# Scores of gated linear attention: three four-way decay steps and a diagonal step with conditional copies, in place of seven two-way levels

## The chip, the core and the metric

The kernel runs on one core of one Trainium2 chip. The metric is device time in microseconds (us). The kernel before takes 827.52 us, the median of three runs (826.87 to 828.48).

Six engines or queues matter here. TensorE is PE, and its weight loads have a row of their own, PEld. VectorE is DVE, ScalarE is ACT and GpSimd is POOL. SyncE is SP, and all large loads are issued from its queue. Each works through its own list of instructions in order, and they meet at semaphores.

## The reference, cut to what matters

One layer of a decoder trunk, 256 tokens wide, model width 2048. `h = RMSNorm(x)` is multiplied by one wide projection, and three attention branches read the parts of the result. Each branch is gated, projected, merged, projected once more and added to x. The part that the change touches is the first branch, gated linear attention (GLA), 4 heads of 128 key dimensions, in chunks of tokens:

```python
b = jnp.cumsum(gi, axis=2)                                   # cumulative log decay, per key dimension
diff = b[:, :, :, None, :] - b[:, :, None, :, :]
decay = jnp.exp(jnp.where(causal[None, None, :, :, None], diff, -jnp.inf))
scores = jnp.einsum('bhid,bhjd,bhijd->bhij', qi, ki, decay)  # for key j <= query i
o_intra = jnp.einsum('bhij,bhje->bhie', scores, vi)
```

A score is the sum over d of q[i,d] k[j,d] exp(b[i,d] - b[j,d]). The exponent depends on i, j and d together, so a plain matmul can't form it. Where a reference token r lies between j and i, the exponential splits in two factors that are both at most 1: exp(b[r] - b[j]) goes to the key and exp(b[i] - b[r]) to the query, and a matmul over d then gives the score.

## The kernel before, in words

**Projections.** The weights are 34 blocks of 2048 x 512, all in fp32. A block is read in four quarters of 1 MB (`w_quarter`, load L129) into one of three buffers named `raw`. Each quarter is split in two halves, and of each half ACT writes the rounded part `hi` (L124) and DVE the remainder `lo` (L125). There are four `hi` and four `lo` buffers. PE then makes three matmuls per product (L166 to L168 for 512 columns, L181 to L184 for 256). One step over 128 of the 2048 rows is a "pull", and it has 6 such matmuls of 512 columns or 12 of 256. A `hi`/`lo` half lasts two pulls.

**Threading.** The attention work isn't a stage of its own. It is written as generators in two lanes, `main` and `side`. After each pull, each lane may emit one step, and a step says how many pulls it lasts. So the instructions of PE are projections with small islands of attention work in them. PE's and SP's instructions stand in the order of the program. For DVE, ACT and POOL a scheduler orders them when the kernel is built, and weights go first (`high_priority`). The `side` lane meanwhile brings the memory tokens: four loads `memT` (L253), split into `m` by ACT L247 and DVE L248, and four loads `memn` (L206) whose squares ACT sums (L207). These loads use the same three `raw` buffers as the weights.

**Scores before** (`gla_scores`). `gB` holds 16 times the cumulative log decay of both token tiles and 4 heads, as 128 dimensions by 1024. It comes from a scan on DVE (L415). `gq` and `gk` hold queries and keys in the same layout. First the scores between the two token tiles are made from `cd` (L448 to L453, matmul L468). The diagonal is a plain product q k of 128 x 128 for each of the 8 head tiles (L460), from which L461 keeps the diagonal. Then come seven levels with s = 64, 32, 16, 8, 4, 2, 1. At each level every 2s tokens are cut into two halves, the last token of the first half is the reference, and second-half queries meet first-half keys. `prep(s)` makes the keys `E` and queries `Q` (DVE L436, L437, ACT exponential L438, DVE L440, L443) one level ahead. PE makes 8 products of 64 columns (L478), DVE multiplies by a mask of 0 and the scale (L480), and adds the result to the score matrix `gA` (L483). A level lasts 11 pulls (`LEVEL_GAP`). After that `gla_out` multiplies the scores by the values (L497, L498).

**After the scores.** The main lane goes on with `gla_out`. The forgetting attention `fox` is put into the lane after the block `fv` is done, and `memory` after the block `mq`. All small matmuls of these parts are in fp32 and go through four PSUM banks named `att`.

Of the kernel before, what the change touches and what calls it, by code (L numbers as in the profile page):

```python
# [24 lines left out]
# columns of w_in  # L25
# [12 lines left out]
# the 512-column blocks in the order in which they are used: (matrix, first column)  # L38
# [9 lines left out]
# columns of the packed constants  # L48
# [6 lines left out]
LEVELS = (64, 32, 16, 8, 4, 2, 1)  # L55
# [4 lines left out]
def body(ctx, tc, xT, memT, xn, memn, wall, wsm, wup, cst, fgain, out):  # L60
# [11 lines left out]
    # the order of the tensor engine's and of the loads' instructions is that of the program  # L72
# [49 lines left out]
    # ------------------------------------------------ weights  # L122
# [34 lines left out]
    def natural(h, kts, wsrc):  # L157
        """psum[t] = h[:, t] @ block: two [128 tokens, 512] banks."""
# [13 lines left out]
    def transposed(h, wsrc, bank=acc):  # L172
        """psum[c] = block columns (tiles 2c, 2c+1) as partitions x 256 tokens."""
# [26 lines left out]
    def rms_of(src, col, stage):  # L200
        """col = rstd as columns [128, NT]."""
# [13 lines left out]
    def row_of(col, row):  # L215
        """row = rstd as a row on every partition [128, S]."""
# [9 lines left out]
    # ------------------------------------------------ constants  # L226
# [12 lines left out]
    # the tensor engine reaches its full clock while the first loads are under way  # L239
# [11 lines left out]
    def load_split(src, tag, gcol, g, h, raw, ks):  # L251
        """Token tiles ks of group g: the gain-scaled transposed input as an exact pair of parts."""
# [17 lines left out]
    def first_w():  # L270
        """The first block and the input with it, in pieces that grow."""
# [22 lines left out]
    xrow = cpool.tile([P, S], F32, name="xrow")  # L294
    mcol = cpool.tile([P, NT], F32, name="mcol")
# [3 lines left out]
    # ------------------------------------------------ the projections  # L299
# [21 lines left out]
    # ------------------------------------------------ constants for later  # L321
# [4 lines left out]
    # masks of the decay levels, carrying the scale of the scores  # L326
    gmask = cpool.tile([P, len(LEVELS), 64], F32, name="gmask")
    nc.gpsimd.memset(gmask, QS)
    for li, s in enumerate(LEVELS):
        nb = 64 // s  # L330
        mk_ = gmask[:, li, :].rearrange("p (b s) -> p b s", s=s)
        nc.gpsimd.affine_select(out=mk_, in_=mk_, pattern=[[-2 * s, nb], [0, s]],
                                compare_op=ALU.is_ge, fill=0.0, base=0, channel_multiplier=1)
        nc.gpsimd.affine_select(out=mk_, in_=mk_, pattern=[[2 * s, nb], [0, s]],
                                compare_op=ALU.is_ge, fill=0.0, base=s - 1, channel_multiplier=-1)
    gdiag = cpool.tile([P, P], F32, name="gdiag")
    nc.vector.tensor_scalar(gdiag, ident, QS, None, ALU.mult)
    # additive causal mask of the two query tiles: [tile 0 | keys 0 | keys 1]
# [7 lines left out]
    # ------------------------------------------------ the 24 small columns  # L346
# [14 lines left out]
    def small_and_norm():  # L361
        """The norm of x; the small columns; the first two blocks' evacuation."""
# [10 lines left out]
        G["q"] = evac_T(gq_ps, xrow)  # L373
# [7 lines left out]
    def log_sigmoid(*args):  # L381
        """dst = min(u, 0) - ln(1 + exp(-|u|)) for each (dst, u, tmp)."""
# [24 lines left out]
        # and the log forget gates of the 8 forgetting heads (rows 32..39)  # L407
# [17 lines left out]
    def gla_scores():  # L425
# [3 lines left out]

        def prep(s):  # L430
# [5 lines left out]
            nc.vector.tensor_tensor(out=Ev[:, :, 0, :], in0=ref, in1=Bv[:, :, 0, :], op=ALU.subtract)  # L436
            nc.vector.tensor_tensor(out=Ev[:, :, 1, :], in0=Bv[:, :, 1, :], in1=ref, op=ALU.subtract)  # L437
            nc.scalar.activation(E, E, AF.Exp, scale=1.0 / 16)  # L438
            Q = a2([P, 8, 64])
            nc.vector.tensor_tensor(out=Q.rearrange("p a (b s) -> p (a b) s", s=s), in0=Ev[:, :, 1, :],  # L440
                                    in1=gqf.rearrange("p (b u s) -> p b u s", u=2, s=s)[:, :, 1, :],
                                    op=ALU.mult)
# [29 lines left out]
        for li, s in enumerate(LEVELS):  # L472
            E, Q = nxt
            if li + 1 < len(LEVELS):
                nxt = prep(LEVELS[li + 1])
# [435 lines left out]
```

## Time and profile before

| what | value |
|---|---|
| median of 3 runs | 827.52 us (826.87 to 828.48) |
| span of the profiled execution, first to last instruction | 824.9 us |
| instructions profiled | 10985 |
| mean granted TensorE clock | 0.997 |
| DVE busy | 488.9 us (59%) |
| ACT busy | 400.5 us (49%) |
| POOL busy | 15.7 us (2%) |
| HBM | 154.39 MB read, 2.10 MB written, 190 GB/s over the span |

The runs shown are 2.6 us longer than the span at their median; the profiled execution has no time listed beside its span, and that difference lies ahead of the first instruction and behind the last. In a row of the timeline the first number is the start in us from the beginning of the span, the second how long the row lasted, and in brackets stands how long the engine had been idle before it and who ended that. On DVE and ACT consecutive instructions overlap a little, so the start-to-start distance is shorter than the duration. A PE row's duration is modelled and also longer than the distance to the next row. An fp32 matmul shows as two instructions ("passes").

### The profile page before, as it was taken

What the parts mean: (1) busy time and instruction counts of PE and PEld (TensorE: products, weight loads), DVE (VectorE), ACT (ScalarE), POOL (GpSimd) and SP (SyncE); (2) the same over time, 40 slices, a digit from 0 to 9 for tenths busy, and PEclk for the clock granted to TensorE, in tenths of its full rate; (3) what the DMA queues carried; (4) which work ended last, traced back from release to release, by engine and by line L of the source; (5) the groups of instructions that cost most, each with busy time, mean ns of one, the idle gap of its engine ahead of it and who ended that gap; (6) DMA issues with size and microseconds to landing.
All of it is one profiled execution on the core that took longest, in us unless ns stands there. A gap on an engine that the chain in (4) does not pass through costs nothing.

```text
span 824.9 us, 10985 instructions
## 1 busy us (share of the span) xinstructions
PE 814.3 (99%) x4470; PEld 708.0 (86%) x4470; DVE 488.9 (59%) x631; ACT 400.5 (49%) x515; POOL 15.7 (2%) x36
## 2 busy tenths in 40 slices
PE   9999999999999999999999999999999999999995
PEld 9998899989899778998888888888888888888885
DVE  6645999665546667666445744474446544566833
ACT  7736765643354456554444444434443444445611
POOL 4000300000000000000000000000000000000000
PEclk9999999999999999999999999999999999999998
DMA  8943466755534344445556545555555555576802
GB/s 316 390 151 125 147 236 226 265 199 165 193 130 173 108 153 154 146 162 182 182 197 204 202 163 197 204 194 170 198 204 194 169 199 204 196 268 249 303 2 103
DMA packets 27363, 157.22 MB, mean 191 GB/s; under 512 B 3216, under 2 KB 4640, under 8 KB 10416
## 3 DMA queue, kind: packets, MB, share of 16 engines
q1 hardware_dynamic: 27040, 156.48, 54.1%
q8 instruction: 35, 0.57, 0.3%
q14 instruction: 16, 0.13, 0.0%
q10 hardware_dynamic: 144, 0.02, 0.0%
q0 software_dynamic: 128, 0.02, 0.0%
HBM read 154.39 MB, written 2.10 MB: 190 GB/s over the span
## 4 chain that ended last, share of the span: by engine, by line
PE 96%; DMA 1%; SPq 1%; DVE 0%; ACT 0%; issue 0%; DVEq 0%; ACTq 0%
PE acc L166 19%; PE acc L168 19%; PE acc L167 19%; PE acc L181 7%; PE acc L183 7%; PE acc L184 7%; PE acc L804 4%; PE acc L803 4%; PE acc L802 4%; DMA raw<-wall 1%; PE att L478 1%; PE att L575 1%; PE att L567 0%; PE att L369 0%; PE att L594 0%; PE att L719 0%
## 5 line engine op out<-in xcount | busy, mean ns | idle before, releaser
L125 DVE TENSOR_TENSOR lo<-raw,hi 128x1024 fp32r<-128x1024 f32 (+2 forms) x269 | 323.3, 1204 | 263.6 <-ACT hi L124 263.5
L124 ACT CAST hi<-raw 128x1024 fp32r<-128x1024 f32 (+2 forms) x269 | 277.8, 1035 | 315.6 <-PE acc L168 214.6
L166 PE MATMUL acc<-hi,x 128*128 128x512 f32 x544 | 215.3, 396 | 0.0
L168 PE MATMUL acc<-hi,x 128*128 128x512 f32 x544 | 211.9, 390 | 0.0
L167 PE MATMUL acc<-lo,x 128*128 128x512 f32 x544 | 211.9, 389 | 0.0
L168 PEld LDWEIGHTS acc<-hi,x 128*128 128x128 f32 x544 | 102.1, 188 | 21.7
L166 PEld LDWEIGHTS acc<-hi,x 128*128 128x128 f32 x544 | 102.2, 188 | 20.9 <-issue 0.5
L167 PEld LDWEIGHTS acc<-lo,x 128*128 128x128 f32 x544 | 102.2, 188 | 20.4
L181 PE MATMUL acc<-x,hi 128*128 128x256 f32 x384 | 110.4, 287 | 0.0
L184 PE MATMUL acc<-x,lo 128*128 128x256 f32 x384 | 108.7, 283 | 0.0
L183 PE MATMUL acc<-x,hi 128*128 128x256 f32 x384 | 108.6, 283 | 0.0
L183 PEld LDWEIGHTS acc<-x,hi 128*128 128x128 f32 x384 | 73.7, 192 | 0.3
L181 PEld LDWEIGHTS acc<-x,hi 128*128 128x128 f32 x384 | 73.6, 192 | 0.3
L184 PEld LDWEIGHTS acc<-x,lo 128*128 128x128 f32 x384 | 73.6, 192 | 0.0
L166 PE MATMUL acc<-hi,oT 128*128 128x512 f32 x128 | 49.8, 389 | 0.0
L167 PE MATMUL acc<-lo,oT 128*128 128x512 f32 x128 | 49.8, 389 | 0.0
L168 PE MATMUL acc<-hi,oT 128*128 128x512 f32 x128 | 49.8, 389 | 0.0
L802 PE MATMUL acc<-hi,a 128*128 128x512 f32 x96 | 37.5, 391 | 0.0
L804 PE MATMUL acc<-hi,a 128*128 128x512 f32 x96 | 37.4, 389 | 0.0
L803 PE MATMUL acc<-lo,a 128*128 128x512 f32 x96 | 37.4, 389 | 0.0
L167 PEld LDWEIGHTS acc<-lo,oT 128*128 128x128 f32 x128 | 24.0, 188 | 5.0
L168 PEld LDWEIGHTS acc<-hi,oT 128*128 128x128 f32 x128 | 24.0, 188 | 5.0
(218 smaller groups left out, 860.2 us busy)
## 6 DMA issues: line engine op xcount, KB each, us to landing
raw<-wall SPq DMA_DIRECT2D x132, 1024.0 KB, 4.8
a<-xn SPq DMA_DIRECT2D x8, 512.0 KB, 7.7
raw<-wall SPq DMA_DIRECT2D x4, 512.0 KB, 7.7
raw<-memT SPq DMA_DIRECT2D x4, 512.0 KB, 3.9
raw<-memn SPq DMA_DIRECT2D x4, 512.0 KB, 5.1
out<-a SPq DMA_DIRECT2D x8, 256.0 KB, 3.2
raw<-wall SPq DMA_DIRECT2D x7, 256.0 KB, 4.3
a<-xT SPq DMA_DIRECT2D x8, 128.0 KB, 4.0
```

The source lines that it names most:

```text
L124: nc.scalar.copy(hi, src)
L125: nc.vector.tensor_tensor(out=lo, in0=src, in1=hi.bitcast(F32), op=ALU.subtract)
L166: MM(ps[t], lhsT=h1, rhs=hi, start=(kt == first), stop=False)
L167: MM(ps[t], lhsT=h1, rhs=lo, start=False, stop=False)
L168: MM(ps[t], lhsT=h2, rhs=hi, start=False, stop=(kt == last))
L181: MM(o, lhsT=w1, rhs=hk[:, 0, :], start=(kt == 0 and c % 2 == 0), stop=False, skip_group_check=True)
L183: MM(o, lhsT=w1, rhs=hk[:, 1, :], start=False, stop=False, skip_group_check=True)
L184: MM(o, lhsT=w2, rhs=hk[:, 0, :], start=False, stop=(kt == KT - 1), skip_group_check=True)
L478: MM(ps[:, e, :], lhsT=E[:, e * P:(e + 1) * P], rhs=Q[:, e, :], start=True, stop=True)
L802: MM(ps, lhsT=h1, rhs=hi, start=(kt == 0), stop=False)
L803: MM(ps, lhsT=h1, rhs=lo, start=False, stop=False)
L804: MM(ps, lhsT=h2, rhs=hi, start=False, stop=(kt == KT - 1))
```

## The change

The seven levels become three four-way steps, s = 32, 8, 2. At each step every 4s tokens are cut into four parts. Each of the first three parts has its last token as reference: its keys carry exp(b[end] - b[j]), and all later parts of the same 4s tokens are its queries. For a head tile of 128 tokens that makes 96 + 64 + 32 = 192 query columns (`Q_N`), in place of 64 at a level before. The keys `E` of all 128 tokens are one subtraction, one exponential and one product (L455, L458, L459 of the changed kernel). The queries are made in two tiles of four head tiles each: three differences (L466), one exponential (L470) and three products (L472) for each. A last step joins neighbours and the diagonal: 64 columns for the odd tokens with the decay from their left neighbour (L485 to L487), and 128 plain query columns, copied by POOL (L488); its keys are the plain `gk`.

A step is 8 products of 192 columns (L522), two to an `att` bank, so it takes all four banks. The scores aren't scaled, masked and added any more. The scale is in the queries already (`qrow`), and a conditional copy on DVE (`copy_predicated`, L536) writes the places where a mask of 0 and 1 is set into `gA`, which POOL has cleared (L503). A step has 12 such copies (4 banks, 3 parts of 192, 128 and 64 elements a partition), the last one 8. The steps still last 11 pulls, so that there are four of them in place of seven levels, and the diagonal's two groups before the first level are gone.

```diff
-LEVELS = (64, 32, 16, 8, 4, 2, 1)
+STEPS = (32, 8, 2)
+Q_OFF = (0, 96, 160)
+Q_N = 192
...
         def prep(s):
-            nb = 1024 // (2 * s)
-            Bv = gB.rearrange("p (b u s) -> p b u s", u=2, s=s)
             E = a4([P, 1024])
-            Ev = E.rearrange("p (b u s) -> p b u s", u=2, s=s)
-            ref = Bv[:, :, 0, s - 1:s].to_broadcast([P, nb, s])
-            nc.vector.tensor_tensor(out=Ev[:, :, 0, :], in0=ref, in1=Bv[:, :, 0, :], op=ALU.subtract)
-            nc.vector.tensor_tensor(out=Ev[:, :, 1, :], in0=Bv[:, :, 1, :], in1=ref, op=ALU.subtract)
+            Bv = gB.rearrange("p (b s) -> p b s", s=s)
+            nc.vector.tensor_tensor(out=E.rearrange("p (b s) -> p b s", s=s),
+                                    in0=Bv[:, :, s - 1:s].to_broadcast([P, 1024 // s, s]), in1=Bv,
+                                    op=ALU.subtract)
             nc.scalar.activation(E, E, AF.Exp, scale=1.0 / 16)
-            Q = a2([P, 8, 64])
-            nc.vector.tensor_tensor(out=Q.rearrange("p a (b s) -> p (a b) s", s=s), in0=Ev[:, :, 1, :],
-                                    in1=gqf.rearrange("p (b u s) -> p b u s", u=2, s=s)[:, :, 1, :],
-                                    op=ALU.mult)
             nc.vector.tensor_tensor(out=E, in0=E, in1=gkf, op=ALU.mult)
-            return E, Q
+            Qs = []
+            for half in range(2):
+                Q = a4([P, 4, Q_N])
+                for b in range(3):
+                    w, nb = (3 - b) * s, 32 // s
+                    end = blocks(gB, half, 4 * s)[:, :, (b + 1) * s - 1:(b + 1) * s]
+                    nc.vector.tensor_tensor(
+                        out=of_q(Q, b, s), in0=later(gB, half, b, s),
+                        in1=end.rearrange("p (e b) s -> p e b s", e=4).to_broadcast([P, 4, nb, w]),
+                        op=ALU.subtract)
+                nc.scalar.activation(Q, Q, AF.Exp, scale=1.0 / 16)
+                for b in range(3):
+                    nc.vector.tensor_tensor(out=of_q(Q, b, s), in0=of_q(Q, b, s),
+                                            in1=later(gqf, half, b, s), op=ALU.mult)
+                Qs.append(Q)
+            return E, Qs
...
-        for c in range(2):
-            ps = att()
-            for e in range(4):
-                sl = slice((4 * c + e) * P, (4 * c + e + 1) * P)
-                MM(ps[:, e * P:(e + 1) * P], lhsT=gkf[:, sl], rhs=gqf[:, sl], start=True, stop=True)
-            nc.vector.tensor_tensor(out=gA[:, 4 * c:4 * c + 4, :], in0=ps.rearrange("p (a b) -> p a b", a=4),
-                                    in1=gdiag.unsqueeze(1).to_broadcast([P, 4, P]), op=ALU.mult)
-            yield 3
-        nxt = prep(LEVELS[0])
+        nc.gpsimd.memset(gA, 0.0)
+        U32 = mybir.dt.uint32
+        yield 6
+        nxt = prep(STEPS[0])
...
-        for li, s in enumerate(LEVELS):
-            E, Q = nxt
-            if li + 1 < len(LEVELS):
-                nxt = prep(LEVELS[li + 1])
-            ps = att().rearrange("p (a b) -> p a b", a=8)
-            for e in range(8):
-                MM(ps[:, e, :], lhsT=E[:, e * P:(e + 1) * P], rhs=Q[:, e, :], start=True, stop=True)
-            T = a2([P, 8, 64])
-            nc.vector.tensor_tensor(out=T, in0=ps, in1=gmask[:, li, :].unsqueeze(1).to_broadcast([P, 8, 64]),
-                                    op=ALU.mult)
-            Av = gA.rearrange("p a (b u s) -> p (a b) u s", u=2, s=s)[:, :, 1, :]
-            nc.vector.tensor_tensor(out=Av, in0=Av, in1=T.rearrange("p a (b s) -> p (a b) s", s=s), op=ALU.add)
+        for li in range(len(STEPS) + 1):
+            E, Qs = nxt
+            if li < len(STEPS):
+                nxt = prep(STEPS[li + 1]) if li + 1 < len(STEPS) else prep_pairs()
+            for c in range(4):
+                ps = att()[:, :2 * Q_N].rearrange("p (a b) -> p a b", a=2)
+                for j in range(2):
+                    e = 2 * c + j
+                    MM(ps[:, j, :], lhsT=E[:, e * P:(e + 1) * P], rhs=Qs[c // 2][:, e % 4, :],
+                       start=True, stop=True)
...
+                for dst, mask, src in parts:
+                    nc.vector.copy_predicated(
+                        dst, mask.bitcast(U32).unsqueeze(1).to_broadcast(list(src.shape)), src)
             yield LEVEL_GAP
```

**Order around the first step.** DVE's instructions from the split of one weight half to the last factor of the first level or step. Names with `lo_`, `hi_` and `raw_` are weights; `a_861` (before) and `a_867` (now) are `gB`. Before, where `a_951` and `b_955` are the keys and queries of the first level:

```order
L125 TENSOR_TENSOR lo_1017<-raw_1010,hi_1016 128x1024 [waits Activation_49]
L436 TENSOR_TENSOR a_1051<-a_861 128x16x32
L440 TENSOR_TENSOR b_955<-a_951,a_787 128x512 [waits Activation_49]
L437 TENSOR_TENSOR a_1051<-a_861 128x16x32
L125 TENSOR_TENSOR lo_1073<-raw_1070,hi_1072 128x1024 [waits DMAHW3_49,Activation_49]
L443 TENSOR_TENSOR a_951<-a_951,a_790 128x1024 [waits DVE_49]
```

Now, where `a_946` (finished earlier) are the keys and `a_950`, `a_958` the two query tiles:

```order
L128 TENSOR_TENSOR lo_1025<-raw_1018,hi_1024 128x1024 [waits Activation_49]
L466 TENSOR_TENSOR a_950<-a_867 128x4x96
L128 TENSOR_TENSOR lo_1106<-raw_1103,hi_1105 128x1024 [waits DMAHW3_49,Activation_49]
L466 TENSOR_TENSOR a_950<-a_867 128x4x64
L466 TENSOR_TENSOR a_950<-a_867 128x4x32
L466 TENSOR_TENSOR a_958<-a_867 128x4x96
L466 TENSOR_TENSOR a_958<-a_867 128x4x64
L466 TENSOR_TENSOR a_958<-a_867 128x4x32
L128 TENSOR_TENSOR lo_1110<-raw_1103,hi_1109 128x1024 [waits Activation_49]
L472 TENSOR_TENSOR a_950<-a_950,a_793 128x4x96 [waits Activation_49]
L472 TENSOR_TENSOR a_950<-a_950,a_793 128x4x64 [waits DVE_49]
L472 TENSOR_TENSOR a_950<-a_950,a_793 128x4x32 [waits DVE_49]
```

Three more products, of `a_958`, follow. Before, 15 DVE instructions follow the scan up to the last factor of the first level; now 22 up to the last product of `a_958`.

**Order of the loads near the end of the block `fk`.** SP's instructions; `memn` are the memory tokens, `wall` the weights. Before:

```order
L129 DMA raw_1551<-wall 128x2048 [waits DMAHW3_49,DVE_49]
L206 DMA raw_1574<-memn 128x1024 [waits DMAHW4_49,DVE_49]
L206 DMA raw_1601<-memn 128x1024 [waits DMAHW5_49,DVE_49]
L129 DMA raw_1616<-wall 128x2048 [waits Activation_49]
L206 DMA raw_1638<-memn 128x1024 [waits Activation_49]
```

Now:

```order
L132 DMA raw_1624<-wall 128x2048 [waits DMAHW2_49,DVE_49]
L209 DMA raw_1647<-memn 128x1024 [waits DMAHW5_49,DVE_49]
L209 DMA raw_1674<-memn 128x1024 [waits Activation_49]
L132 DMA raw_1689<-wall 128x2048 [waits DMAHW6_49,DVE_49]
L209 DMA raw_1711<-memn 128x1024 [waits DMAHW4_49,DVE_49]
```

The loads are the same, in the same order. What moved is which of the three buffers each one takes, and so what it waits for. In the built program the weight load after the second `memn` load (`raw_1616` before, `raw_1689` now) waited for ACT's squares of a `memn` buffer; now it waits for DVE's split `lo_1631`, the last reader of `raw_1624`.

**DVE around that load,** now:

```order
L251 SCALAR_TENSOR_TENSOR m_186_1543<-raw_1544,cs,m_186_1543 128x256 [waits DMAHW4_49]
L251 SCALAR_TENSOR_TENSOR m_186_1543<-raw_1544,cs,m_186_1543 128x256 x2
L128 TENSOR_TENSOR lo_1631<-raw_1624,hi_1630 128x1024 [waits PE_49,Activation_49]
L251 SCALAR_TENSOR_TENSOR m_186_1543<-raw_1544,cs,m_186_1543 128x256
L128 TENSOR_TENSOR lo_1692<-raw_1689,hi_1691 128x1024 [waits DMAHW1_49,PE_49,Activation_49]
```

Between the split that frees the buffer and the split of the weights that are loaded into it stands one instruction. At the same place before:

```order
L483 TENSOR_TENSOR a_877<-a_877,b_1455 128x32x16 [waits DVE_49]
L443 TENSOR_TENSOR a_1641<-a_1641,a_790 128x1024 [waits DVE_49]
L125 TENSOR_TENSOR lo_1558<-raw_1551,hi_1557 128x1024 [waits PE_49,Activation_49]
L125 TENSOR_TENSOR lo_1619<-raw_1616,hi_1618 128x1024 [waits DMAHW1_49,PE_49,Activation_49]
L125 TENSOR_TENSOR lo_1623<-raw_1616,hi_1622 128x1024 [waits PE_49,Activation_49]
```

and the splits of `m`, which now stand here, came 13 instructions earlier.

More of the change, by code (lines that the diff above doesn't have):

```diff
@@ L294, in body @@
     xrow = cpool.tile([P, S], F32, name="xrow")
+    qrow = cpool.tile([P, S], F32, name="qrow")
     mcol = cpool.tile([P, NT], F32, name="mcol")
@@ L372, in small_and_norm @@
         yield from row_of(xcol, xrow)
-        G["q"] = evac_T(gq_ps, xrow)
+        nc.vector.tensor_scalar(qrow, xrow, QS, None, ALU.mult)
+        G["q"] = evac_T(gq_ps, qrow)
         G["k"] = evac_T(gk_ps, xrow)
@@ new lines, in prep, with prep_pairs @@
+            return E, Qs
+        def prep_pairs():
+            Qs = []
+            for half in range(2):
+                Q = a4([P, 4, Q_N])
+                Bh, qh = blocks(gB, half, 2), blocks(gqf, half, 2)
+                odd = Q[:, :, :64]
+                pick = lambda v, u: v[:, :, u].rearrange("p (e b) -> p e b", e=4)
+                nc.vector.tensor_tensor(out=odd, in0=pick(Bh, 1), in1=pick(Bh, 0), op=ALU.subtract)
+                nc.scalar.activation(odd, odd, AF.Exp, scale=1.0 / 16)
+                nc.vector.tensor_tensor(out=odd, in0=odd, in1=pick(qh, 1), op=ALU.mult)
+                nc.gpsimd.tensor_copy(Q[:, :, 64:], gqf[:, 512 * half:512 * half + 512].rearrange(
+                    "p (e i) -> p e i", e=4))
+                Qs.append(Q)
+            return gkf, Qs
```

45 lines of the change are left out of this document (33 added, 12 removed).

## The prediction

> **What bounds the kernel now.** I read the page first: span, busy times and the chain of work that ended last.
>
> ```profile
> span 824.9 us, 10985 instructions
> PE 814.3 (99%) x4470; PEld 708.0 (86%) x4470; DVE 488.9 (59%) x631; ACT 400.5 (49%) x515; POOL 15.7 (2%) x36
> PE 96%; DMA 1%; SPq 1%; DVE 0%; ACT 0%; issue 0%; DVEq 0%; ACTq 0%
> ```
>
> PE is the bound from end to end: 96% of the chain. An instruction taken from PE shortens the span by its length, and a wait that PE gets lengthens it by its length. DVE has room on average. The question is whether it has room where the scores are made, so the next view is the table of stretches (PE, weight loads, DVE, ACT, POOL, each with its count):
>
> ```profile
> 84.00:106.00 22.00, 22.00 (x111) 18.63 (x110) 21.89 (x28) 14.73 (x20) 6.92 (x10) 1.00 0.44 155
> 106.00:134.00 28.00, 28.00 (x232) 27.77 (x231) 26.09 (x37) 18.71 (x27) 0.00 (x0) 1.00 0.63 214
> 134.00:160.00 26.00, 26.00 (x215) 25.77 (x215) 17.55 (x27) 16.62 (x22) 0.00 (x0) 1.00 0.81 290
> ```
>
> From 84 to 134 us DVE is busy for 48 of 50 us; its average of 59% says nothing about this place. The clock is 1.00 throughout.
>
> **PE: what goes and what comes.** The timeline of PE around a diagonal group, a level, and a group of fp32 products of 256 columns:
>
> ```profile
> 74.09 1.05 PE L460 MATMUL att<-a,a 128*128 128x128 f32 x8
> 74.90 0.48 PE L166 MATMUL acc<-hi,x 128*128 128x512 f32 x1
> 75.22 0.39 PE L167 MATMUL acc<-lo,x 128*128 128x512 f32 x1
> 99.95 1.89 PE L478 MATMUL att<-b,a 128*128 128x64 f32 x16
> 101.65 0.48 PE L166 MATMUL acc<-hi,x 128*128 128x512 f32 x1
> 101.97 0.39 PE L167 MATMUL acc<-lo,x 128*128 128x512 f32 x1
> 225.23 1.02 PE L498 MATMUL att<-a,a 128*128 128x256 f32 x4
> 225.90 0.58 PE L166 MATMUL acc<-hi,m 128*128 128x512 f32 x1
> 226.32 0.40 PE L167 MATMUL acc<-lo,m 128*128 128x512 f32 x1
> 102.20 0.40 PE L168 MATMUL acc<-hi,x 128*128 128x512 f32 x1
> ```
>
> The projections run at 0.23 us from start to start (101.97 to 102.20). A level occupies 99.95 to 101.65 and makes the next matmul 0.32 - 0.23 = 0.09 later: 1.79 us, and seven levels are 12.5 us. A diagonal group is 0.81 + 0.09 = 0.90, two are 1.8 us. Removed: 14.3 us.
>
> A pass of 192 columns isn't in the trace. With 64 columns it is 1.79/16 = 0.112 us, with 128 columns 0.90/8 = 0.112, with 256 columns (0.67 + 0.19)/4 = 0.215. So above 128 columns the columns set it. I take 192/256 of the last, 0.161 us; the bounds are 0.112 and 0.215. Added are 4 steps x 8 products x 2 passes = 64 passes: 10.3 us, with 0.1 for entering and leaving 10.4. **PE saves 3.9 us** (bounds 7.1 and 0.5). The rest of PE's work stands in another order and is the same.
>
> **DVE: the first step.** The timeline of DVE from the scan that makes `gB`, and three sizes for the costs:
>
> ```profile
> 85.29 2.29 DVE L415 TENSOR_TENSOR_SCAN a<-a,a 128x1024 f32<-128x1024 f32 x1
> 93.58 0.69 DVE L437 TENSOR_TENSOR a<-a 128x512 f32<-128x512 f32 x1
> 94.19 1.22 DVE L125 TENSOR_TENSOR lo<-raw,hi 128x1024 fp32r<-128x1024 f32 x1
> 95.32 0.69 DVE L436 TENSOR_TENSOR a<-a 128x512 f32<-128x512 f32 x1
> 98.26 1.22 DVE L443 TENSOR_TENSOR a<-a,a 128x1024 f32<-128x1024 f32 x1
> 100.54 0.48 DVE L248 SCALAR_TENSOR_TENSOR m<-raw,cs,m 128x256 fp32r<-128x256 f32 x1
> 100.93 0.69 DVE L440 TENSOR_TENSOR b<-a,a 128x512 f32<-128x512 f32 x1
> 26.46 0.43 DVE L356 TENSOR_TENSOR a<-wsr,a 128x128 fp32r<-128x128 f32 x2
> L569 DVE COPY b<-att 128x384 f32<-128x384 f32 x8 | 4.5, 557 | 4.5 <-PE att L567 4.5
> ```
>
> From start to start 1024 elements take 1.13 us (94.19 to 95.32), 512 take 0.61, an `m` split 0.39, 128 take 0.21, and 384 take 0.557 less the overlap of 0.08, 0.48. Between these I set 256 at 0.34, 192 at 0.27 and 64 at 0.14. The scan ends at 87.58. The order then lists up to the last product of the first step: five weight splits (5.65), three instructions of 512 for `cd` (1.8), two of 1024 for the keys (2.27), six differences and six products of the queries (2 x 2 x (0.48 + 0.34 + 0.21) = 4.1). That is 13.8 us, so the second query tile is ready at 101.4 and the first, three products earlier, at 100.4. Before, the first level's last factor is ready at 99.48 and PE comes at 99.95. Now PE comes 1.8 us earlier, at 98.15, and **waits 2.3 us**. Both halves together last 2.6 us, so the second tile makes no further wait.
>
> **DVE: the loads behind it.** A step costs DVE 2.27 + 4.1 = 6.4 us for its factors and 4 x (0.27 + 0.21 + 0.14) = 2.5 us for its copies, if a conditional copy costs what a two-input instruction of its size costs. That is 8.9 us every 18.5 us of PE, where a level cost 5 x 0.61 + 1.13 = 4.2 every 17.6. The trace has no conditional copy: below these rows it can't well be, since it reads source and mask; I bound it above by twice the row, and take the row.
>
> What this delays: the splits of the memory tokens stand behind the copies, and DVE frees the three `raw` buffers. I follow it to the place where the margin ends, the load `raw_1689`. From 101.4 to the end of the split `lo_1573` DVE has 12 weight splits (13.6), two further steps' factors (12.7), 24 copies (5.0), 12 `m` splits (4.7), four of 512 for the block `fq` (2.4) and three of the pairs (1.0): 39.4 us, so 140.8 at the earliest. On the way it also waits for loads that were issued late, behind an `m` split; I put that at 2 us: 142.8. From here on transfers set the pace:
>
> ```profile
> L207 ACT ACTIVATE raw<-raw 128x1024 f32<-128x1024 f32 x4 | 4.2, 1061 | 2.9 <-DMA raw<-memn 2.9
> raw<-wall SPq DMA_DIRECT2D x132, 1024.0 KB, 4.8
> raw<-memn SPq DMA_DIRECT2D x4, 512.0 KB, 5.1
> 119.50 0.33 SPq L129 DMA_DIRECT2D raw<-wall  x1
> 124.41 1.05 ACT L124 CAST hi<-raw 128x1024 fp32r<-128x1024 f32 x1 [0.27 <-DMA raw<-wall]
> 139.51 0.33 SPq L129 DMA_DIRECT2D raw<-wall  x1
> 145.94 1.05 ACT L124 CAST hi<-raw 128x1024 fp32r<-128x1024 f32 x1 [2.56 <-DMA raw<-wall]
> ```
>
> `raw_1647` (memory tokens) takes the buffer that `lo_1573` frees and lands about 4.9 us later, at 147.7. ACT's square of it stands ahead of the cast `hi_1630`: 1.0 + 1.0, 149.7; `lo_1631` 1.2 more, 150.9. Only then may SP issue `raw_1689`. A weight load was on ACT after 4.9 us when alone (119.50 to 124.41) and after 6.4 among `memn` loads (139.51 to 145.94); I take 5.5: 156.4. Cast 1.05, split 1.22: `lo_1692` is there at 158.7.
>
> When PE wants it follows from the spacing now:
>
> ```profile
> 117.30 1.90 PE L478 MATMUL att<-b,a 128*128 128x64 f32 x16
> 119.00 0.36 PE L181 MATMUL acc<-x,hi 128*128 128x256 f32 x1
> 119.32 0.28 PE L184 MATMUL acc<-x,lo 128*128 128x256 f32 x1
> 119.44 0.28 PE L181 MATMUL acc<-x,hi 128*128 128x256 f32 x1
> 134.92 1.90 PE L478 MATMUL att<-b,a 128*128 128x64 f32 x16
> ```
>
> Step 0 ends at 100.4 + 2.6 = 103.0. The stretches of projections between levels are 15.65 (101.65 to 117.30) and 15.92 (119.00 to 134.92), a step 2.6: step 2 ends at 103.0 + 15.65 + 2.6 + 15.92 + 2.6 = 139.8. Five weight halves of 24 matmuls at 0.12 follow, 14.5 with the entry, and the third matmul of the sixth is the first that reads `lo_1692`: 154.5. **PE waits 4.2 us.** The memory loads and splits behind that are late by as much, but PE is too, and after the last step DVE has no more scores to make, so I count no third wait.
>
> **Sum.** 824.9 - 3.9 + 2.3 + 4.2 = 827.5 us of span. The median of the runs is 2.6 above the span (827.52), and nothing outside the span changes: **830.1 us**. From `gla_out` on, attention work comes about 33 pulls earlier (three levels of 11); PE has no gap there before, so an earlier place gains nothing.
>
> Removed at no gain: DVE's masks and additions (0.69 us each) and 14 mask instructions on POOL. Added at no cost: 18 smaller mask instructions and a clearing on POOL, in its idle time before 84 us and at 85; the scaled row `qrow`, 0.3 us on DVE ahead of a scan that POOL's and ACT's work times; and ACT's longer exponentials, 1.06 a level (as L207's row of 1024 elements) and now 1.06 + 2 x 0.8 a step (three quarters of it each), on an engine busy 15 of 22 us; without that cover each would add its 0.8 to the first step.
>
> **Rivals.**
>
> *Hidden after all (faster).* The late load decides from the point where `lo_1692` comes before 154.5. If DVE's waits of 2 us don't arise and `raw_1647`'s square isn't what holds `lo_1631`, DVE reaches its end after two more weight splits, 12 copies, three `m` splits and one product of the pairs (2.3 + 2.5 + 1.2 + 0.3) at 147.1; a load of 4.8 then gives 147.1 + 4.8 + 1.05 + 1.22 = 154.2, and PE waits only at the first step: 830.1 - 4.2 = 825.9. For it: from 84 to 160 us DVE is busy for 65.5 of 76 us, and the change puts 3 x 8.9 + 1.4 = 28 us there in place of six levels' factors (2.96 each) and five times mask and addition (1.2 each), 24 us; it still fits. Against: `m` splits and the loads they free now stand behind that work in the order. Without the first wait too it is 823.6.
>
> *Copies dear (slower still).* At twice the row 24 copies add 5.0 us to the way to `lo_1573`: 835.1. For it: three streams, source, mask, target. Against: all two-input rows follow their element count, whatever their shape.
>
> *POOL in the way.* The two query copies on POOL (L488) run beside DVE's two-input work. What the trace shows of such a pair:
>
> ```profile
> 1.60 0.65 POOL L332 TENSOR_SCALAR_AFFINE_SELECT gmask<-gmask 128x64 f32<-128x64 f32 x3
> 4.99 0.92 POOL L332 TENSOR_SCALAR_AFFINE_SELECT gmask<-gmask 128x64 f32<-128x64 f32 x1
> ```
>
> The same POOL instruction took 0.22 us with DVE idle and 0.92 with DVE splitting weights, so one holds up the other. If instead POOL comes first, DVE stands for the copy, at most 0.95 each by this row, twice: 832.0. The Trainium skill, "SBUF — State Buffer", section "SBUF: two separate sides", says that a DVE instruction with two SBUF inputs and a GpSimd instruction that reads SBUF lock each other out for a whole instruction, whichever starts first; the trace agrees for POOL's side, and no run here shows DVE's.
>
> *The products don't get cheaper.* If a pass of 192 columns takes the 0.215 of 256, PE saves 0.5 and not 3.9: 833.5.
>
> **How the numbers follow.** The forecast has a chance of 0.50, with a range of its own from 828.3 to 833 (load 4.8 to 6.4, DVE's waits 1 to 3). Hidden after all has 0.28, copies dear 0.10, POOL in the way 0.06, no cheaper products 0.06. About 0.2%, 1.7 us, is what a measurement can tell from no change: 825.9 to 829.2 is "same". Hidden lies on that edge: 0.17 faster, 0.11 same. Of the forecast 0.10 falls under 829.2 and 0.40 above; the other three are slower, 0.22. Faster 0.17, same 0.21, slower 0.62. The range goes from 825.0, where half of the hidden case is left out, to 834.5, just short of copies at twice the row.
>
> **What would show it.** In the changed profile: L522 at 2.6 us a step, 10.3 in all; PE idle about 2 us before the first L522, ended by DVE L472; PE idle about 4 us at the end of block `fk`, ended by DVE's `lo` or ACT's `hi` behind a DMA; DVE busy over 95% from 84 to 140 us; L536 at 0.2 to 0.35 us. Wrong it would be if PE shows no second wait, or if waits appear in `fox` and `memory`, which I take to be free of them.

## The result, and the profile after

The changed kernel takes 832.52 us (832.32 to 833.38) where the kernel before, on the same chip, takes 827.40 (826.87 to 828.48): the ratio is 1.0064, with a 95% interval from 1.0052 to 1.0076. It is slower by 5.1 us. The forecast was 830.1, slower, with a range from 825.0 to 834.5.

The page of the changed kernel, the same three lines as before:

```profile
span 831.2 us, 10924 instructions
PE 814.2 (98%) x4406; PEld 706.7 (85%) x4406; DVE 488.5 (59%) x677; ACT 396.9 (48%) x515; POOL 18.3 (2%) x44
PE 85%; DVE 6%; DMA 4%; ACT 2%; issue 1%; SPq 1%; POOL 0%; DVEq 0%; ACTq 0%
```

PE has fallen from 96% of the chain to 85%; DVE, transfers and ACT now hold 12% of it. The table of stretches (PE, weight loads, DVE, ACT, POOL, each with its count, then granted clock, DMA share, GB/s) says where:

```profile
84.00:106.00 22.00, 20.11 (x96) 16.62 (x95) 21.92 (x30) 16.70 (x22) 3.58 (x5) 1.00 0.37 123
106.00:134.00 28.00, 28.00 (x216) 27.37 (x215) 26.97 (x62) 16.57 (x23) 3.80 (x6) 1.00 0.49 170
134.00:160.00 26.00, 21.75 (x173) 21.24 (x171) 17.59 (x40) 10.92 (x17) 1.93 (x3) 0.98 0.60 203
```

Before, PE was busy in all 76 us; now 6.1 us are missing, in two places. The timeline of PE at both, with the second score step, which is undisturbed, between them:

```profile
99.11 0.39 PE L171 MATMUL acc<-hi,x 128*128 128x512 f32 x1
101.33 2.84 PE L522 MATMUL att<-a,a 128*128 128x192 f32 x16 [1.83 <-ACT m L250]
...
119.57 2.77 PE L522 MATMUL att<-a,a 128*128 128x192 f32 x16
122.03 0.41 PE L184 MATMUL acc<-x,hi 128*128 128x256 f32 x1
122.29 0.28 PE L186 MATMUL acc<-x,hi 128*128 128x256 f32 x1
...
154.87 0.28 PE L187 MATMUL acc<-x,lo 128*128 128x256 f32 x1
158.93 0.39 PE L184 MATMUL acc<-x,hi 128*128 128x256 f32 x1 [3.78 <-ACT hi L127]
...
160.19 0.58 PE L187 MATMUL acc<-x,lo 128*128 128x256 f32 x1 [0.66 <-DVE lo L128]
160.57 0.42 PE L184 MATMUL acc<-x,hi 128*128 128x256 f32 x1
...
162.49 4.50 PE L522 MATMUL att<-a,a 128*128 128x192 f32 x16
166.69 0.41 PE L184 MATMUL acc<-x,hi 128*128 128x256 f32 x1
```

The first wait: 101.33 is 2.22 after 99.11, and a projection matmul takes 0.23, so PE stood 2.0 us. Its label, ACT's L250, is wrong: that instruction has no part in the step. In the kernel below that moves all memory work, L250 isn't at this place any more, and the same wait is as long and has another label. What the step needs is the third of the six products of the queries (L472); the second and third of them end on DVE at 100.56 + 0.62 = 101.18:

```profile
100.56 0.62 DVE L472 TENSOR_TENSOR a<-a,a 128x256 f32<-128x256 f32 x2
PE att L522 <- ACT hi L127: 1.8, 1, 1.8
```

The first row is of the changed kernel, the second is the wait of the kernel with the memory work moved. The second wait: 154.87 to 160.57 is 5.7 us for what takes four times 0.12 when nothing is late: 5.2 us lost to a half of the weights that is late. Behind it comes something that the prediction does not have: from 160.57 to 162.49 nine projection matmuls take 0.213 each where 0.12 is usual, and the last score step 4.20 where the second took 2.46. The table of stretches around it shows the clock:

```profile
154.00:158.00 4.00, 1.15 (x10) 0.95 (x8) 0.00 (x0) 1.16 (x3) 0.00 (x0) 1.00 0.89 282
...
160.00:162.00 2.00, 1.81 (x8) 1.81 (x9) 1.27 (x2) 1.93 (x4) 0.00 (x0) 0.50 0.29 45
...
164.00:166.00 2.00, 2.00 (x7) 2.00 (x7) 0.77 (x5) 1.17 (x3) 0.00 (x0) 0.50 0.99 418
166.00:168.00 2.00, 2.00 (x16) 2.00 (x16) 2.00 (x8) 1.94 (x2) 0.00 (x0) 1.00 1.04 438
```

The granted clock falls to 0.50 after PE has stood, and stays there until about 166 us: 0.8 us on the nine matmuls and 1.7 on the step, 2.6 together (0.84 and 1.74).

At the other end of the span there is a difference that the prediction doesn't have either. From PE's last projection matmul to the end of the span it was 9.5 us before (from 815.41) and is 8.7 now (from 822.49). What ACT and DVE do there is the same; the output transfers land sooner (first row before, second now, last number: median us from issue to landing):

```profile
out<-a SPq DMA_DIRECT2D x8, 256.0 KB, 3.2
out<-a SPq DMA_DIRECT2D x8, 256.0 KB, 2.4
```

All twelve kernels with the new scores that were profiled show 2.4 and 8.7; the two with the old ones show 3.2 and 3.1, and 9.5. Why the landing is shorter isn't shown.

| between the two profiled executions | us |
|---|---|
| scores on PE at full clock: 4 steps of 2.60 (2.46, and 0.14 at the exit) for 14.3 | -3.9 |
| first wait | +2.0 |
| second wait | +5.2 |
| half clock behind it | +2.6 |
| first 50 us (PE's matmuls with the weights' small columns, L376, start at 50.80; before, L369, at 49.96) | +0.8 |
| behind PE's last projection matmul: 8.7 for 9.5 | -0.8 |
| sum, against 831.2 - 824.9 = 6.3 | 5.9 |

The chain of waits of the changed kernel, from the issue of `raw_1647` to PE, is the chain that the prediction follows (start, length, what); it ends at PE's L187 at 160.19:

```profile
143.82 3.96 DMA raw<-memn
147.87 1.16 ACT raw L210 x2
149.02 0.94 ACT hi L127
149.99 1.24 DVE lo L128
151.24 6.51 DMA raw<-wall
157.83 1.05 ACT hi L127
158.91 1.24 DVE lo L128
```

### The profile page after: what moved, and what is told of

Its sections match the earlier page's. It is cut to its first block, busy times and chain, and to the rows that moved or that the text cites. A ratio compares the mean times of both kernels' runs of the same rounds, so it can differ in the third digit from the quotient of the medians.

```text
span 831.2 us, 10924 instructions
## 1 busy us (share of the span) xinstructions
PE 814.2 (98%) x4406; PEld 706.7 (85%) x4406; DVE 488.5 (59%) x677; ACT 396.9 (48%) x515; POOL 18.3 (2%) x44
## 4 chain that ended last, share of the span: by engine, by line
PE 85%; DVE 6%; DMA 4%; ACT 2%; issue 1%; SPq 1%; POOL 0%; DVEq 0%; ACTq 0%
PE acc L171 18%; PE acc L169 18%; PE acc L170 18%; PE acc L187 5%; PE acc L184 5%; PE acc L186 5%; DMA raw<-wall 4%; PE acc L857 4%; PE acc L856 4%; PE acc L858 4%; DVE lo L128 3%; ACT hi L127 1%; PE att L629 1%; PE att L522 1%; DVE a L472 1%
## 5 line engine op out<-in xcount | busy, mean ns | idle before, releaser
L187 PE MATMUL acc<-x,lo 128*128 128x256 f32 x384 | 109.4, 285 | 0.7 <-DVE lo L128 0.7
L187 PEld LDWEIGHTS acc<-x,lo 128*128 128x128 f32 x384 | 74.2, 193 | 1.0 <-DVE lo L128 1.0
```

The source lines that it names most:

```text
L187: MM(o, lhsT=w2, rhs=hk[:, 0, :], start=False, stop=(kt == KT - 1), skip_group_check=True)
```

## The experiments

The theory at this point: the weight half that PE waits for at 155 us is late because its load stands in SP's order behind the memory tokens' loads; and a PE that stands for some 4 us pays a second time in clock. All runs are of the changed kernel with the edit shown, unless it says otherwise. "Before" is the kernel before on the same chip.

### Is the half clock a consequence of standing?

```diff
-            yield LEVEL_GAP
+            if li == 2:
+                yield 10
+                idle = att()
+                for _ in range(16):
+                    MM(idle[:, :P], lhsT=ones, rhs=ones, start=True, stop=True)
+                yield 1
+            else:
+                yield LEVEL_GAP
```

> Adds 16 fp32 products of 128 columns on constant data (their result is used nowhere) on PE directly ahead of the matmul that waits 3.9 us for hi_1691. Theory (a PE that stands for some 4 us is granted half its clock afterwards, which made the 16 passes of the last score step 4.2 us instead of 2.5 and nine projection matmuls 0.21 instead of 0.12): 16 x 0.224 = 3.6 us of work go into the wait, the granted clock stays at 1.00 from 154 to 168 us, the last step takes about 2.5, and the time falls by about 2.7 us, to 829.8. Rival (the clock falls there for another reason, such as the transfers or the work of that stretch): the clock still falls, the time stays at 832.5 or rises. Rival (the filler displaces work): up to 836.

830.33 us (829.55 to 830.85), ratio to before 1.0033 (1.0020 to 1.0045). Work was added to the engine that bounds the kernel, and the kernel got 2.2 us faster. The timeline of PE and a row of the stretches:

```profile
154.87 3.73 PE L542 MATMUL att<-ones 128*128 128x128 f32 x32
159.97 0.38 PE L187 MATMUL acc<-x,lo 128*128 128x256 f32 x1 [0.75 <-DVE lo L128]
...
161.25 2.77 PE L522 MATMUL att<-a,a 128*128 128x192 f32 x16
```

```profile
160.00:162.00 2.00, 2.00 (x15) 2.00 (x16) 1.28 (x3) 1.98 (x5) 0.00 (x0) 1.00 0.31 49
```

The filler covers 3.7 us of the wait, the rest of the wait is as long as before, the clock stays at 1.00 and the last step is back at its usual length. The half clock is a consequence of standing, and its price is about 2.2 us of time (2.6 in the table, from one profile).

The same edit with 4 products in place of 16 leaves a shorter stand:

> As the kernel with the filler ahead of the matmul that waits for hi_1691, but 4 products and not 16: 0.9 us of work, so that PE stands for about 3.0 us in one piece and not 3.9 or 0. PE stood 2.0 us ahead of the first score step and kept its clock; it stood 3.6 to 3.9 and lost half of it. If the clock falls after 3.0 us of standing: 832.5, last score step over 3 us. If it doesn't: 830.3 as with 16 products, last score step 2.5 us.

832.99 us (832.19 to 833.72), ratio 1.0065 (1.0051 to 1.0079): no gain. PE stood 3.4 us in one piece, and the last step took 3.96 us by its row, where the second step of the changed kernel has 2.77:

```profile
159.37 0.58 PE L184 MATMUL acc<-x,hi 128*128 128x256 f32 x1 [3.36 <-ACT hi L127]
...
162.93 3.96 PE L522 MATMUL att<-a,a 128*128 128x192 f32 x16
```

```profile
158.00:160.00 2.00, 0.63 (x2) 0.50 (x2) 0.65 (x1) 1.73 (x2) 0.00 (x0) 0.63 0.73 299
```

So by the rows' own figures 1.8 us of standing (the first wait, in every run that has it) kept the clock and 3.4 lost it. The Trainium skill, "TensorE: Matmul & The Clock Gate", section "Part 1: The HAM clock gate", says that the clock goes to half after an idle window of about 3.4 us and that the window runs freely, whenever the work starts. The trace agrees with it at both lengths, but not in the moment: here the granted clock is at 0.50 from 158.5 us (0.63 is the mean of its row), 2.5 us after the filler's last product, and in the kernel with the later first step below it fell 2.1 us after PE's last matmul. So standing of 2 us isn't shown to be safe everywhere.

### Where does the second wait come from?

The loads for the norm of the memory tokens are put 12 pulls later on the side lane:

```diff
+    side.append(gap(12))
     side.append(rms_of(
         memn, mcol, lambda: wpool.tile([P, 1024], F32, tag="raw", name=nm("raw"), bufs=3)))
```

> The four loads of the memory tokens for their norm start 12 pulls later on the side lane; nothing else moves. Theory (the weight half for the end of block fk is late because its load stands on SP behind the memory tokens' loads and waits for the split behind their square on ACT): its load is issued at about 144 us and not 151, the half is ready at about 152.6, ahead of PE's 154.9; second wait (5.1) and clock loss (2.7) both go, the first wait of 2.0 stays: 824.7. Rival (DVE's backlog of factors and copies makes the split late whatever SP's order is): the wait at 155 us stays at 4 us or more, 831 to 833. Rival (the wait goes to where the moved loads stand, before block mk): about 829.

824.81 us (824.38 to 826.11), ratio 0.9967 (0.9954 to 0.9980): 7.7 us less than the changed kernel, as forecast, and faster than before. The longest of PE's waits (the other two that its profile lists, 1.1 and 0.4 us, are at the start), and SP's queue:

```profile
PE att L522 <- ACT m L250: 1.8, 1, 1.8
```

```profile
134.04 15.79 SPq L132 DMA_DIRECT2D raw<-wall  x5
151.77 7.22 SPq L209 DMA_DIRECT2D raw<-memn  x2
```

The second wait and the half clock are gone, the first wait is as it was. DVE has the same work as before: the order of the loads, with the buffers they wait for, made the half late, not DVE's backlog alone.

The same edit on the kernel before, as a control:

> The kernel before, with only the memory tokens' loads for their norm 12 pulls later. Theory (PE had no wait there before, so the loads' place costs nothing): 827.3, within 0.2%. Rival (the place of these loads costs time in itself, whatever the scores do, so that what their move gained in the changed kernel says nothing of the change): 825 or less.

827.17 us (826.59 to 828.12), ratio 0.9996 (0.9987 to 1.0005): no difference. The place of these loads costs nothing until the scores push DVE's splits behind it. The other moves below weren't tried on the kernel before; its profile has one wait of PE, 1.1 us at the start, so they would have had none in this stretch to remove.

### Does the first wait cost by itself?

The cross product stays, and the first score step comes two pulls later on PE:

```diff
         nc.scalar.copy(gX, ps.rearrange("p (a b) -> p a b", a=4))
-        yield 3
+        yield 5
```

> The first score step stands two pulls (12 projection matmuls, 2.7 us) later on PE, its factors where they are. Theory (the second wait is set by a chain of loads that does not depend on when PE gets there): the first wait of 2.0 us goes, PE comes to the late weight half 2.0 us earlier and waits 2.0 us longer there: 832.5, within half a microsecond. Rival (the two waits are separate costs): 830.5.

830.07 us (829.16 to 831.80), ratio 1.0034 (1.0025 to 1.0044): 2.4 us faster, where I had expected nothing. The timeline of PE says why, and that the rival isn't right either:

```profile
101.04 2.76 PE L522 MATMUL att<-a,a 128*128 128x192 f32 x16
...
117.76 0.28 PE L187 MATMUL acc<-x,lo 128*128 128x256 f32 x1
121.64 0.58 PE L184 MATMUL acc<-x,hi 128*128 128x256 f32 x1 [3.60 <-ACT hi L127]
...
122.90 0.58 PE L187 MATMUL acc<-x,lo 128*128 128x256 f32 x1 [0.46 <-DVE lo L128]
```

```profile
120.00:122.00 2.00, 0.36 (x1) 0.36 (x2) 0.82 (x3) 1.46 (x2) 0.00 (x0) 0.53 0.88 305
```

The second view is a row of the stretches: the clock falls here too. The first wait is gone, and so is the one at 155 us. In their place PE waits 5.0 us at 118 us, for an earlier half of the weights. In the changed kernel that half was split at 122.87, and PE came to it at 123.60 (12 matmuls behind the step that ends at 122.03) and to the first matmul that reads the split at 123.84: 1.0 us of margin that nothing had shown. Without the first wait (2.0) and with the second step now behind it (2.6), PE comes 4.6 us earlier than it did, and the half's load took 5.95 us where it had taken 4.92. Having waited there, PE finds the half at 155 us in time. My reading is that DVE and its loads are late by some 5 us in this stretch and that PE pays this once, at the half that it first meets too early; the two places, 5.2 and 5.0 us, fit it.

Both edits together:

> The first score step two pulls later and the memory tokens' loads 12 pulls later, together. Theory: both waits and the clock loss go, 832.5 - 2.0 - 5.1 - 2.7 = 822.7, which is the time before less the 3.9 us that PE saves in the scores and within 0.8 of it. The weight half (152.6) has little margin against PE (152.9), so up to 1 us may be left of the second wait: 822.5 to 824. Rival (DVE is the bound of the whole stretch): 828 or more, with PE waiting for DVE in the score steps.

829.99 us (829.10 to 831.66), ratio 1.0033 (1.0023 to 1.0042). The expectation failed by 7 us, for the same reason: the wait is at 118 us, ahead of the place that the moved loads relieve.

```profile
PE acc L184 <- ACT hi L127: 3.7, 1, 3.7
```

Each removed wait must therefore be removed with the loads of its own place. The memory tokens' transposed loads and their 16 splits on DVE stand in the whole stretch (the loads are issued from 96 to 130 us, the last split ends at 151.6), so all memory work is moved now, first alone and then with the later first step:

```diff
+    side.append(gap(12))
     side.append(load_mem())
```

> All work on the memory tokens, their transposed loads and splits and then the loads for their norm, starts 12 pulls later on the side lane; the first score step stands where the change put it. Theory (the second wait came from the memory tokens' loads in SP's order and their splits on DVE): no second wait and no clock loss as when only the norm's loads moved, and the first wait stays at about 2 us since the weight splits and factors ahead of it are the same: 824 to 825. Rival (what the memory tokens leave free doesn't help, DVE's score work alone is too much): a wait of 4 us or more between 115 and 160 us, 829 to 832. Rival (the moved work is late for its own user, block mk): a wait of PE near 205 us, 826 or more.

> As the kernel with all memory work 12 pulls later, and the first score step two pulls later on PE. With the first step later but the memory tokens' splits in place, PE had waited 5 us at 118 us for a weight half whose load stood behind those splits and the copies. Theory (it is the memory tokens' part in that stretch that makes the half late): that wait is gone too, no wait is left over 1 us, 822.5 (the time before less about 4 for the scores, with at most 1 more). Rival (the score steps' factors and copies alone fill DVE there): the wait at 118 us stays at 3 to 5 us, 827 to 830.

Alone it is 824.94 us (824.46 to 826.05), ratio 0.9972 (0.9962 to 0.9981), with the first wait of 2.0 left: the same as moving only the norm's loads. With the later step it is 823.96 (822.73 to 825.45), ratio 0.9957 (0.9943 to 0.9971), and no wait at 118 us: where both edits of the run above met that wait, this one does not, and the difference between them is the memory tokens' transposed part. A short wait of 0.6 us is left at 180 us, behind the norm's loads.

### How much does DVE's work count?

Each conditional copy of the three steps is issued twice:

```diff
-                for dst, mask, src in parts:
+                for dst, mask, src in parts + (parts if li < len(STEPS) else []):
```

> The changed kernel with each conditional copy of the three steps issued twice (the second places the same values): 36 more on DVE, 24 of them ahead of the end of lo_1573, at 0.27, 0.20 and 0.13 us each from start to start, 4.8 us. Theory (DVE works without a break in that stretch and every microsecond on it delays the late weight half as much): the second wait grows from 5 to nearly 10 us, 837. Rival (the copies stand in DVE's gaps, the loads alone set the half): 833 or less.

835.14 us (835.09 to 835.20), ratio 1.0091 (1.0077 to 1.0105): 2.6 us more, not 4.8, so the theory's one-to-one price fails. The wait also moved:

```profile
140.57 1.54 PE L522 MATMUL att<-a,a 128*128 128x192 f32 x8 [1.61 <-DVE a L536]
146.31 1.90 PE L522 MATMUL att<-a,a 128*128 128x192 f32 x8 [4.19 <-DVE a L536]
```

PE is held up before it comes to the late half. It stands inside the third step, where the four `att` banks are still held by the copies of earlier products, 5.8 us in two pieces, and loses its clock there too. The half at 155 us is then ready in time. So DVE's work counts, but through whatever it releases last; with copies at this price the banks become the limit.

The two copies of the queries are put on ACT in place of POOL:

```diff
-                nc.gpsimd.tensor_copy(Q[:, :, 64:], gqf[:, 512 * half:512 * half + 512].rearrange(
+                nc.scalar.copy(Q[:, :, 64:], gqf[:, 512 * half:512 * half + 512].rearrange(
```

> The changed kernel with the two copies of the queries (512 columns each) on ACT in place of POOL. Two weight splits on DVE beside them took 1.52 and 1.63 us where 1.22 is usual. Theory (POOL's copy holds DVE up, by 0.3 and 0.4 us, and both splits lie on the way to the late weight half): the two splits take 1.22, the second wait gets 0.7 shorter: 831.8. Rival (the lengthening comes from something else or is made up before): splits of 1.5, or no change of time: 832.5. Rival (two copies of 0.5 more on ACT delay its casts): 833.

Two weight splits on DVE, first in the changed kernel, then in this one:

```profile
121.35 3.07 DVE L128 TENSOR_TENSOR lo<-raw,hi 128x1024 fp32r<-128x1024 f32 x2 [0.29 <-ACT hi L127]
```

```profile
120.21 2.36 DVE L128 TENSOR_TENSOR lo<-raw,hi 128x1024 fp32r<-128x1024 f32 x2 [0.20 <-ACT hi L127]
```

The splits are back at 1.22 each, so a POOL copy did hold DVE up, by 0.7 us in all. In the time it doesn't show: 832.01 us (831.10 to 833.01), ratio 1.0056 (1.0041 to 1.0071), and 1.0064 (1.0052 to 1.0076) for the changed kernel; the intervals overlap.

### The start, and the best order found

> The changed kernel with masks for the first step alone: 6 of the 18 mask instructions on POOL stay, and the masks of the other two steps are left all ones, so that their copies place everything (the scores of those steps are not the reference's; the instructions that run after the start are the same). The changed kernel's runs have 2.2 us outside the span, those of before 1.7, and its first 50 us were 0.8 longer in the profiled run. Theory (the start's 0.8 is scatter of its transfers, POOL's masks stand beside nothing that sets the end): 832.5, outside the span still 2.2. Rival (the masks cost time at the start or in front of it): up to 1.3 less, 831.2, and 1.7 outside the span.

832.16 us (831.23 to 833.49), ratio 1.0056 (1.0042 to 1.0070): not to be told from the changed kernel. The start's 0.8 us is scatter: PE's small columns (L376) begin between 49.6 and 52.0 us in eleven profiles of kernels with all the masks, and at 50.0 here. One part of the rival is right, though. The time outside the span falls from 2.2 us to 1.73 with 12 instructions fewer on POOL.

Last, all edits that helped, with the norm's loads another 8 pulls later:

> The changed kernel with the first score step two pulls later, the memory tokens' work 12 pulls later and the loads for their norm 8 more, and the two copies of the queries on ACT. No wait is left from 84 to 180 us (the kernel with the first two of these edits had one of 0.6 us at 180 us behind the norm's loads): 823.2, between 822.5 and 824.0. Rival (the norm's loads, put later again, meet the weights of block mk): a wait of PE between 190 and 215 us, 824.5 or more.

822.94 us (822.35 to 823.63), ratio to before 0.9942 (0.9928 to 0.9955): 4.5 us faster than the kernel before. All waits of PE in its profile:

```profile
PE att L187 <- DVE lo L128: 1.2, 3, 0.8
PE att L245 <- DVE ones L237: 1.1, 1, 1.1
PE att L184 <- ACT hi L127: 0.4, 1, 0.4
PE acc L187 <- DVE lo L128: 0.2, 1, 0.2
```

Only the start's waits (the first three rows, all in the first 20 us) and 0.2 us are left. Once the loads beside it stand elsewhere, the change of the scores pays. Not all of the 4.5 us is PE's: from the first matmul with the small columns to PE's last projection matmul the profile has 762.1 us where the kernel before has 765.4: 3.3 less, where 3.9 was forecast for the scores. Another 0.8, behind it, is the outputs' earlier landing.

## Why the prediction was right or wrong

The sign and the mechanism were right, the time was 2.4 us short, inside the range. Part of its nearness is luck: two terms that the sum lacks, the clock and the outputs' landing, go opposite ways. By its own steps:

- **PE saves 3.9.** 3.9 at full clock was measured: a step is 2.60 us and four are 10.4, as forecast. Two deviations cancel in it: a pass of 192 columns takes 2.46/16 = 0.154 us against the 0.161 taken, and leaving the steps costs 0.14 each, 0.56 and not 0.1. The rival that the products don't get cheaper falls.
- **The first wait, 2.3.** 2.0 was measured. The term was right; the page's label for the releaser (ACT's L250, where L472 was foretold) shows why such labels need the program beside them.
- **DVE's prices.** A conditional copy takes what a two-input instruction of its size takes, as taken: the rows of the changed kernel's DVE show 0.27 from start to start for 192 elements. Copies dear falls.

```profile
110.67 0.36 DVE L536 COPY_PREDICATED a<-gmask,att 128x192 f32<-128x192 uint32 x1
110.94 1.21 DVE L128 TENSOR_TENSOR lo<-raw,hi 128x1024 fp32r<-128x1024 f32 x1
```

- **The second wait, 4.2.** 5.2 was measured, at the place, on the engine and by the chain foretold: `raw_1647` was issued at 143.8 (142.8 was forecast), `raw_1689` at 151.2 (150.9), PE came at 155.0 (154.5). These times hold the late start's 0.8, and on the way the memory tokens' load took 4.0 where 4.9 was taken, which made up for a buffer that came free late. The term that was mis-sized is the load of the weights, 6.5 us against the 5.5 taken, between two loads of the memory tokens.
- **What the sum left out: the clock.** The prediction priced a wait at its length. A wait of over 3 us cost PE 2.2 us more (the filler's run), which is most of the miss. The trace of before has no stand of PE inside its dense part, so no row priced it. It did show the fall: PE's last projection matmul starts at 815.41, and some 4 us later the granted clock goes to 0.50 (its mean over the microsecond below is 0.82, and 0.50 over the next). Neither that row nor the rule cited above was weighed.

```profile
819.00:820.00 1.00, 0.00 (x0) 0.00 (x0) 0.15 (x1) 0.00 (x0) 0.00 (x0) 0.82 0.79 289
```

- **"Nothing outside the span changes."** It does: 1.7 us in the runs of before, 2.2 in those of the changed kernel, 0.5 of the miss. The 2.6 that I took was the profiled execution against the median, of which 0.9 is scatter inside the span. The end of the span changes too, by -0.8 (the outputs' landing), and hides as much of the miss. Against the forecast change of 2.6 us, the clock (2.6), the load (1.0), the first wait (-0.3), these two (0.5 and -0.8) add 3.0; the medians differ by 2.5 more.
- **Two waits as two terms.** The sum treated them as additive with PE's arrival carried through, and that is right for this order. But the first wait was also a cover for a half at 118 us with 1.0 us to spare, which the prediction didn't follow; it shows only when the first wait is taken away.
- **POOL in the way.** Seen (0.7 us on two splits), without a measured effect on the time. **Hidden after all** falls in the given order; with the loads moved it comes out at 822.9, near the 823.6 that it gave for no waits.
- **No waits in `fox` and `memory`:** right, PE's list of waits has none there.

What stays open: why the time outside the span goes with the number of POOL's instructions, why the outputs land sooner, and the last 0.4 us of the table.

## What to carry to other kernels

Where work on the bounding engine gets shorter, follow every load behind the helper engines' longer work, in the order of the issuing queue, to the place where its margin is least, and then ask which margin is next: here some 5 us turned up at 118, at 139 to 146 or at 155 us, depending on what was changed. Take the loads that nobody needs yet out of that stretch before judging the change; the same edit to the scores was 0.6% slower with them in it, and 0.6% faster with them and the first step put later. And price a wait of PE like those here (3.4 us or more; between 1.8 and 3.4 nothing was tried) at its length plus the half clock behind it.

## What the runs showed of the hardware that was not expected

- Standing and clock: PE kept its full clock after standing 1.8 us and lost half of it after 3.4 (4 products of filler), 3.6 (the later first step) and 3.8 us (the changed kernel). The fall came 2.5, 2.1 and 4.0 us after PE's last matmul, so its moment isn't tied to the start of the stand. The half clock lasted 6.8 us in these three, and 3.4 in the kernel with both edits (a stand of 3.7) and in the one with each copy twice (4.2). Filling the stand with 3.7 us of useless products made the kernel 2.2 us faster.
- The time outside the span was 1.7 us for the kernel before (36 instructions on POOL) and for the one with few masks (32), 2.0 for the two with both query copies on ACT (42), and 2.2 for the changed kernel (44).
- A POOL copy of 512 elements made the DVE split beside it longer, by 0.3 and 0.4 us in the two cases. The copies' rows are 0.6 and 0.9 long; the first had 0.44 us left when the split began (121.18 + 0.61 against 121.35), and the second began while a split was running, so part of its row may itself be waiting.
